# A layer's output stage: who turns the gated attention rows, TensorE or a transposing DMA, and roots taken for two row tiles at once

## The chip, the cores and the metric

The kernel runs on one core of one Trainium2 chip. The metric is device time in microseconds (us) of one execution; the median of three runs is given. A core has TensorE (PE in the profile; its weight loads are PEld), VectorE (DVE), ScalarE (ACT), GpSimd (POOL) and the queue engine SyncE (SP), which here issues most transfers. Each engine runs its own instructions in order; they wait for one another through semaphores.

## The reference, cut to what matters

A hybrid decoder layer for 2048 positions of width 1024. Two attention branches (8 heads with a forget gate, 8 heads in a sliding window) fill one row `o` of 1024 values for each position. The last stage then gates, projects, normalises and adds:

```
oa = oa * silu(za); ob = ob * silu(zb)
y = concatenate([oa, ob], axis=-1) @ w_out      # 2048x1024 @ 1024x1024
x = x + gate * rms_norm(y, g_post)              # root over the 1024 values of a row
```

## The kernel before, in words

All products are made in half precision parts: a number is split into a high f16 part and the f16 rest, and three matmuls (high-high, high-low, low-high) stand for one.

The attention leaves its rows in memory tensor `o_d` (positions by channels) and the gates in `z_d` (channels by positions, 8 blocks of 128). The output stage works in 16 row tiles of 128 positions, class `Out`, one object `outs[t]` for each. A tile's life:

- `load` (SP queue): `z` (L1457) and then `o` (L1451), 512 KB each, into quarters of the buffer `T`, two tiles in rotation.
- `turn`: eight 128x128 TensorE transposes (L1463) put `o`, channels first, into two PSUM banks. Then, each some ticks later: `gate` (DVE, L1472, two multiplies of 512 columns, PSUM times `z`, into `z`), `squares_` (ACT, L1475, sum of squares of `z`), `scale_` (a TensorE matmul with `ones` to add over partitions, L1479, then the two small DVE operations of `root_scale`, L112 and L113), the high part (ACT, L1485) and the low part (DVE, L1486) of the scaled `z`, which are the stationary operand `hl` (tile `oz`) of the product.
- `product(n, k)`: half `n` (512 output columns) of the product, for channel block `k`; three matmuls of 512 columns (L1499). 16 such units make a tile: 48 matmuls. After unit `k` = 7 of a half, `evac`: ACT squares the PSUM bank with a row sum (L1507), DVE multiplies it with the gate row into `y` (L1515).
- `root`: fifteen DVE operations on one column (`unscale` L1525 and L1526, L1543 and L1544, `rsqrt_mean` L92 to L106 with three Newton steps, L1546). `store`: one DVE operation over 1024 columns (L1553) adds `x`, and SP writes 512 KB out (L1554). `x` is loaded at the first unit of the second half (L1496).

The order is written out by hand. `ounits` lists the units: the products of tiles 0 and 1, then for each tile t from 2 on the 16 products in order, with `turn` of tile t+1 behind the third. `after(n, f)` puts `f` into a list; each `tick()` counts the entries down and calls those that are due, in the order in which they were put there. In the final part a tick follows every second unit. Python order is instruction order on each engine:

```
def tick():
    now = [f for n, f in late if n <= 1]
    late[:] = [[n - 1, f] for n, f in late if n > 1]
    for f in now:
        f()
```

The first `N_IN` = 33 units (tiles 0 and 1 and the turn of tile 2) are mixed into the last head of the attention; the rest, from tile 2 on, run alone. "Host tile" below is the tile whose products run while the turn of the next tile goes on in their midst.

`rsqrt_mean(dst, ss, n)` works on `n` columns; its Newton step is two operations for `n` = 1 and three for larger `n`. Another place of the kernel, the sliding window attention, already uses transposing DMAs: `Pair.split` writes a high and a low f16 part of 128x1024 and sends each through `SP.dma_start_transpose` (L908, L913).

Of the kernel before, what the change touches and what calls it, by code (L numbers as in the profile page):

```python
# [15 lines left out]
ALU = mybir.AluOpType  # L16
AX = mybir.AxisListType

P = 128
# [21 lines left out]
def hybrid_layer(  # L41
# [1347 lines left out]
    def open_out():  # L1389
# [9 lines left out]
        def rotate(key, views):  # L1399
            n = [0]  # L1400

            def next_():
                n[0] += 1
                return views[n[0] % 2]

            oio[key] = next_
# [6 lines left out]
        rotate("x", oxy[:2])  # L1413
        rotate("y", oxy[2:])
        oio["w"] = wo.tile([P, 2, KT, D], F16, name="wohl")
# [20 lines left out]
    class Out:  # L1436


        def __init__(self, t):
            self.t = t  # L1440
            self.last = t == NB - 1
            self.cuts = (0, CH, CH + 3 * P, D) if self.last else (0, CH, D)

# [9 lines left out]
        def load_z(self):  # L1453
# [3 lines left out]
            SP.dma_start(self.z, z_d[:, :, rows_].rearrange("k p n -> p k n"))  # L1457

        def turn(self, lag):

            px = [bk[bank()][:].rearrange("p (k n) -> p k n", k=4) for _ in range(2)]
            for k in range(KT):
                PE.transpose(px[k // 4][:, k % 4, :], self.o[:, k * P:(k + 1) * P], ident[:])  # L1463
            self.hl = wpool.tile([P, 2, KT, P], F16, tag=("whl", "wraw")[self.t % 2], name="oz")
            self.sc = sm(1, "w_pw")
            hi, lo = self.hl[:, 0], self.hl[:, 1]
            gs = sm(1, "w_mx")

            def gate():
                for h in range(2):  # L1470
                    z = self.z[:, 4 * h:4 * h + 4, :]
                    V.tensor_tensor(z, px[h], z, op=ALU.mult)  # L1472

# [3 lines left out]
            def scale_():  # L1477
                pg = bk[bank()][:, 0:1]
                PE.matmul(pg, ones[:], gs[:], start=True, stop=True)  # L1479
                root_scale(self.sc[:], pg)  # L1480

            after(1, gate)
            after(2, squares_)
            after(lag, scale_)
            after(lag + 1, lambda: A.activation(hi, self.z, AF.Copy, scale=self.sc[:]))  # L1485
            after(lag + 2, lambda: V.scalar_tensor_tensor(lo, self.z, self.sc[:], hi, op0=ALU.mult, op1=ALU.subtract))  # L1486

        def product(self, n, k):
            cc = slice(self.cuts[n], self.cuts[n + 1])
            if k == 0:  # L1490
                self.b = bank(True)
                if n == 0:
                    self.ss = sm(4, "y_ss")
                elif n == 1:
                    self.x = oio["x"]()
                    SP.dma_start(self.x[:], xs[self.t * P:(self.t + 1) * P, :])  # L1496
            py, b = bk[self.b][:, :cc.stop - cc.start], self.b
# [21 lines left out]
            if n == len(self.cuts) - 2:  # L1519
                after(2 if self.last else 4, self.root)  # L1520
                after(2 if self.last else 7, self.store)

        def unscale(self):
            self.inv = sm(1, "w_sw")
            V.tensor_tensor(self.inv[:], self.sc[:], ysc[:], op=ALU.mult)  # L1525
            V.reciprocal(self.inv[:], self.inv[:])  # L1526
# [8 lines left out]
        def root(self):  # L1535
# [4 lines left out]
            else:  # L1540
# [5 lines left out]
                V.tensor_tensor(rst[:], rst[:], inv[:], op=ALU.mult)  # L1546
            self.rst = rst

        def store(self):
            y, rst = self.y, self.rst  # L1550
            for n, e in enumerate((SP, A) if self.last else (SP,)):
                cc = slice(n * CH, (n + 1) * CH) if self.last else slice(0, D)
                V.scalar_tensor_tensor(y[:, cc], y[:, cc], rst[:], self.x[:, cc], op0=ALU.mult, op1=ALU.add)  # L1553
                e.dma_start(os_[self.t * P:(self.t + 1) * P, cc], y[:, cc])  # L1554
# [4 lines left out]
    for t, n in [(0, 0), (1, 0), (0, 1), (1, 1)] + [(t, n) for t in range(2, NB) for n in range(len(outs[t].cuts) - 1)]:  # L1559
        if n == 0 and t + 2 < NB:  # L1560
            oloads[len(ounits)] = t + 2
        for q in range(KT):
            ounits.append(lambda t=t, n=n, q=q: outs[t].product(n, q))
            nxt = 2 if (t, n) == (0, 1) else t + 1 if n == 0 and 2 <= t < NB - 1 else None
            if q == 2 and nxt:
                ounits.append(lambda nxt=nxt: outs[nxt].turn(4))
    opos = [0]
    N_IN = 4 * KT + 1

# [156 lines left out]
```

## Time and profile before

| | |
|---|---|
| median of 3 runs (lowest, highest) | 1167.06 us (1166.04, 1169.31) |
| the profiled execution | 1165.92 us, span 1164.2 us |
| mean granted TensorE clock | 0.995 |
| busy share of the span | PE 96%, DVE 79%, ACT 58%, POOL 14% |
| TensorE operations L1463 in the last stage | 128x128, f32 |
| bytes of one execution | 136.36 MB over DMA, 117 GB/s in the mean |

The span reaches from the first to the last instruction; the rest of the execution's time lies around it. Busy time of PE is no measure of the end by itself, since matmuls overlap; the chain of work that ended last says where time passes.

### The profile page before, as it was taken

Reading aid. Unit: us, or ns where it says so; the run is one execution under the profiler, and the core shown is the slowest. Engines: PE = TensorE matmul, PEld = TensorE weight load, DVE = VectorE, ACT = ScalarE, POOL = GpSimd, SP = SyncE. Lnnn points to the kernel's source line nnn. Section 1 sums busy time; section 2 is a strip of 40 time slices with the busy share of each in tenths; the row PEclk is TensorE's granted clock in tenths of the full one; section 3 lists DMA queues with packets and bytes.
Section 4 is the critical chain, followed back from the end, with each engine's and each line's share of the span. In section 5 each row is a group of like instructions: output and inputs, shape, how many; then the busy total and the mean of one; then the engine's idle time right before and its main releaser. Section 6 shows DMA issues by size and latency. Waiting matters only on the chain. (4 is left out here: it accounts for less than half of the span.)

```text
span 1164.2 us, 27013 instructions
## 1 busy us (share of the span) xinstructions
PE 1116.3 (96%) x10514; PEld 652.8 (56%) x10514; DVE 915.9 (79%) x2330; ACT 677.9 (58%) x1124; POOL 166.0 (14%) x302
## 2 busy tenths in 40 slices
PE   5899999999999999999999999999999989999997
PEld 1466557544469955555555555555555555555554
DVE  6776578889878757789988889878897886767665
ACT  4666445656545534767766667777676688323332
POOL 2011223233332201111111111002000000000000
PEclk9999999999999999999999999999999999999999
DMA  9645446576766622333233232313112255454642
GB/s 330 219 139 166 106 76 134 116 162 129 147 134 130 123 64 69 85 83 79 74 77 92 73 79 74 68 42 94 45 45 49 60 169 172 150 201 166 211 165 89
DMA packets 162452, 136.36 MB, mean 117 GB/s; under 512 B 95356, under 2 KB 139428, under 8 KB 162324
## 3 DMA queue, kind: packets, MB, share of 16 engines
q1 hardware_dynamic: 152388, 106.39, 34.8%
q0 software_dynamic: 9456, 27.72, 8.9%
q8 instruction: 82, 1.34, 0.5%
q10 hardware_dynamic: 480, 0.53, 0.2%
q14 instruction: 46, 0.38, 0.1%
HBM read 70.97 MB, written 25.18 MB: 83 GB/s over the span
## 5 line engine op out<-in xcount | busy, mean ns | idle before, releaser
L1331 ACT ACTIVATE p<-sta,lift,scl_qk 128x1024 f32<-128x1024 f32 (+2 forms) x160 | 171.8, 1074 | 94.7 <-PE sta L1327 88.9
L334 PE MATMUL bk<-hT,wh_qk 128*128 128x512 f16 x768 | 197.9, 378 | 0.6 <-DVE a_m L1280 0.6
L1499 PE MATMUL bk<-wohl,oz 128*128 128x512 f16 (+2 forms) x792 | 172.5, 372 | 2.2 <-DVE oz L1486 1.0
L1342 DVE TENSOR_TENSOR pha<-p,pha 128x1024 f16<-128x1024 f32 (+2 forms) x160 | 169.8, 1061 | 0.0
L1339 ACT ACTIVATE pha<-p 128x1024 f16<-128x1024 f32 (+2 forms) x160 | 148.1, 925 | 31.6 <-POOL p L1335 26.8
L1280 DVE TENSOR_REDUCE a_m<-bk 128x1 f32<-128x512 f32 x192 | 129.4, 684 | 36.2 <-PE bk L1277 35.3
L1499 PEld LDWEIGHTS <-oz 128*128 128x128 f16 x792 | 75.8, 99 | 83.2 <-issue 1.8
L1352 PE MATMUL poa<-vt,pha 128*128 128x65 f16 x1088 | 116.5, 193 | 1.6 <-DVE ona L1361 1.6
L1355 PE MATMUL poa<-vt,pha 128*128 128x65 f16 x1088 | 116.0, 192 | 1.4 <-DVE pha L1342 1.4
L1354 PE MATMUL poa<-vt,pha 128*128 128x64 f16 x1088 | 116.3, 194 | 0.0
L1326 PE MATMUL sta<-T 128*128 128x512 f16 (+1 forms) x320 | 109.6, 347 | 4.5 <-ACT p L1331 4.5
L1277 PE MATMUL bk<-T 66*128 66x512 f16 (+2 forms) x320 | 110.5, 348 | 2.1 <-DVE a_m L1280 2.1
L1352 PEld LDWEIGHTS <-pha 128*128 128x128 f16 x1088 | 101.6, 97 | 16.3 <-DVE ona L1361 2.9
L334 PEld LDWEIGHTS <-wh_qk 128*128 128x128 f16 x768 | 70.2, 97 | 71.6 <-issue 2.9
L1354 PEld LDWEIGHTS <-pha 128*128 128x128 f16 x1088 | 101.0, 97 | 13.4
L1327 PE MATMUL sta<-T 69*128 69x512 f16 (+1 forms) x320 | 108.0, 348 | 0.0
L1355 PEld LDWEIGHTS <-pha 128*128 128x128 f16 x1088 | 100.8, 99 | 1.6 <-DVE pha L1342 1.6
L334 PE MATMUL bk<-hT,wh_za 128*128 128x512 f16 x384 | 99.9, 379 | 0.0
L352 PE MATMUL bk<-wh_va,hT 128*128 128x128 f16 x1536 | 94.1, 221 | 0.0
L352 PEld LDWEIGHTS <-hT 128*128 128x128 f16 x1536 | 89.1, 99 | 6.1 <-issue 3.3
L334 PE MATMUL bk<-hT,wh_zb 128*128 128x512 f16 x384 | 91.2, 379 | 1.0 <-DVE wh_zb L278 1.0
L1335 POOL TENSOR_SCALAR_AFFINE_SELECT p<-p 128x256 f32<-128x256 f32 x64 | 31.9, 499 | 413.4 <-ACT p L1331 408.5
(497 smaller groups left out, 1857.0 us busy)
## 6 DMA issues: line engine op xcount, KB each, us to landing
hT<-in_x_dram SPq DMA_DIRECT2D x20, 512.0 KB
wa<-in_w_ada_dram SPq DMA_DIRECT2D x16, 512.0 KB
T<-stq SPq DMA_DIRECT2D x128, 64.0 KB
T<-z_d SPq DMA_DIRECT2D x16, 512.0 KB
T<-o_d SPq DMA_DIRECT2D x16, 512.0 KB
z_d<-tz POOLq DMA_DIRECT2D x30, 256.0 KB, 2.9
out_dram<-hT SPq DMA_DIRECT2D x15, 512.0 KB
xt<-in_x_dram SPq DMA_DIRECT2D x12, 512.0 KB
```

What stands on the lines that cost most here:

```text
L334: PE.matmul(ps, whl[:, a, k, :], hT[ci][:, b, k, :], start=(k == 0 and n == 0), stop=(k == KT - 1 and n == 2))
L352: PE.matmul(ps[:, u * P:(u + 1) * P], hT[ci][:, a, k, u * P:(u + 1) * P], whl[:, b, k, :], start=(k == 0 and n == 0), stop=(k == KT - 1 an ...
L1277: PE.matmul(mx[:, :w], T[0:XM, 0, i * P:(i + 1) * P], T[0:XM, 2, pc * CH:pc * CH + w], start=True, stop=True)
L1280: V.tensor_reduce(m3[:, u, pc:pc + 1], mx[:, :w], axis=AX.X, op=ALU.max)
L1326: PE.matmul(self.st[:, o:o + w], T[:, 3, kb_], T[:, 1, qc], start=True, stop=False)
L1331: A.activation(self.p32[:, :self.w], self.st[:, :self.w], AF.Exp, scale=scl[f"qk{self.hd}"][:], bias=lift[:])
L1339: A.activation(self.ph[:, 0, :self.w], self.p32[:, :self.w], AF.Copy)
L1342: V.tensor_tensor(self.ph[:, 1, :self.w], self.p32[:, :self.w], self.ph[:, 0, :self.w], op=ALU.subtract)
L1352: PE.matmul(po[:, u, :], ph[:, 0, pq], vt[:, b, hd, 0:65], start=(self.first and n == 0 and u == 0), stop=False)
L1354: PE.matmul(po[:, u, 0:64], ph[:, 0, pq], vt[:, b, hd, 65:VW], start=False, stop=False)
L1355: PE.matmul(po[:, u, :], ph[:, 1, pq], vt[:, b, hd, 0:65], start=False, stop=(self.last and n == len(self.blocks) - 1))
L1499: PE.matmul(py, self.hl[:, i, k, :], w_slot(8 * j + k)[:, cc], start=(k == 0 and m_ == 0), stop=(k == KT - 1 and m_ == 2))
```

## The change: what it does

For tiles 3 to 15, `turn` issues no TensorE transposes. A new unit, `split` of tile t+2, stands behind the second product unit of the second half of tile t (t from 1 to 13): ACT copies `o` into a f16 high part, DVE subtracts it from `o` for the f16 low part (at the next tick), and SP sends each part, 128x1024, through a transposing DMA into one half of a buffer `tt`; both are two tiles in rotation, as views of the tile `spare`. `gate` becomes two DVE operations over 1024 columns: `o` = high + low (f16 and f16, f32 out), then `z` = `o` * `z`.

For tiles 2 to 13, the roots are taken in pairs (`pair_root`, 3 ticks after the odd tile's last product; 19 DVE operations on two columns, `rsqrt_mean` with `n` = 2), and the two stores follow 5 and 7 ticks after that product. Both tiles' `x` loads are issued in the odd tile, and `y` gets a third buffer. `N_IN` is 34, since `split` of tile 3 lies in the mixed part. With `split`, a tile has 18 units, so 9 ticks.

```diff
--- before.py
+++ after.py
@@ -1401,7 +1401,7 @@
 
             def next_():
                 n[0] += 1
-                return views[n[0] % 2]
+                return views[n[0] % len(views)]
 
             oio[key] = next_
 
@@ -1411,7 +1411,10 @@
         oio["r"] = [spare[:, 2 * CH * n:2 * CH * (n + 1)].bitcast(F32) for n in range(6)]
         oio["j"] = [spare[:, CH * a:CH * b].bitcast(BF16) for a, b in ((12, 14), (14, 15), (15, 16))]
         rotate("x", oxy[:2])
-        rotate("y", oxy[2:])
+        rotate("y", oxy[2:] + [gz[:]])
+        turned = [spare[:, 4 * CH * n:4 * CH * (n + 1)].rearrange("p (a k q) -> p a k q", a=2, k=KT) for n in range(2)]
+        rotate("t", turned)
+        oio["s"] = spare[:, 8 * CH:12 * CH].rearrange("p (a n) -> p a n", a=2)
         oio["w"] = wo.tile([P, 2, KT, D], F16, name="wohl")
 
         fm = sm(1, "w_p2")
@@ -1439,6 +1442,7 @@
         def __init__(self, t):
             self.t = t
             self.last = t == NB - 1
+            self.paired = 2 <= t < NB - 2
             self.cuts = (0, CH, CH + 3 * P, D) if self.last else (0, CH, D)
 
         def load(self):
@@ -1456,20 +1460,40 @@
             self.z = Ts[0][:, 2 + t % 2, :].bitcast(F32).rearrange("p (k n) -> p k n", k=KT)
             SP.dma_start(self.z, z_d[:, :, rows_].rearrange("k p n -> p k n"))
 
+        def split(self):
+            hl, self.tt = oio["s"], oio["t"]()
+
+            def low():
+                V.tensor_tensor(hl[:, 1, :], self.o, hl[:, 0, :], op=ALU.subtract)
+                SP.dma_start_transpose(self.tt[:, 1], hl[:, 1, :])
+
+            A.activation(hl[:, 0, :], self.o, AF.Copy)
+            SP.dma_start_transpose(self.tt[:, 0], hl[:, 0, :])
+            after(1, low)
+
         def turn(self, lag):
 
-            px = [bk[bank()][:].rearrange("p (k n) -> p k n", k=4) for _ in range(2)]
-            for k in range(KT):
-                PE.transpose(px[k // 4][:, k % 4, :], self.o[:, k * P:(k + 1) * P], ident[:])
+            mate = self.t - 1 if 2 < self.t < NB - 2 and self.t % 2 else None
+            self.pair = outs[mate].pair if mate else (sm(4, "b_m"), sm(4, "b_nb"))
+            e = self.t % 2
             self.hl = wpool.tile([P, 2, KT, P], F16, tag=("whl", "wraw")[self.t % 2], name="oz")
-            self.sc = sm(1, "w_pw")
+            self.sc = self.pair[0][:, e:e + 1] if self.paired else sm(1, "w_pw")[:]
             hi, lo = self.hl[:, 0], self.hl[:, 1]
             gs = sm(1, "w_mx")
+            if self.t < 3:
+                px = [bk[bank()][:].rearrange("p (k n) -> p k n", k=4) for _ in range(2)]
+                for k in range(KT):
+                    PE.transpose(px[k // 4][:, k % 4, :], self.o[:, k * P:(k + 1) * P], ident[:])
 
             def gate():
-                for h in range(2):
-                    z = self.z[:, 4 * h:4 * h + 4, :]
-                    V.tensor_tensor(z, px[h], z, op=ALU.mult)
+                if self.t < 3:
+                    for h in range(2):
+                        z = self.z[:, 4 * h:4 * h + 4, :]
+                        V.tensor_tensor(z, px[h], z, op=ALU.mult)
+                else:
+                    o = self.o.rearrange("p (k n) -> p k n", k=KT)
+                    V.tensor_tensor(o, self.tt[:, 0], self.tt[:, 1], op=ALU.add)
+                    V.tensor_tensor(self.z, o, self.z, op=ALU.mult)
 
             def squares_():
                 A.activation(oio["j"][0].rearrange("p (k n) -> p k n", k=KT), self.z, AF.Square, accum_out=gs[:])
@@ -1477,23 +1501,24 @@
             def scale_():
                 pg = bk[bank()][:, 0:1]
                 PE.matmul(pg, ones[:], gs[:], start=True, stop=True)
-                root_scale(self.sc[:], pg)
+                root_scale(self.sc, pg)
 
             after(1, gate)
             after(2, squares_)
             after(lag, scale_)
-            after(lag + 1, lambda: A.activation(hi, self.z, AF.Copy, scale=self.sc[:]))
-            after(lag + 2, lambda: V.scalar_tensor_tensor(lo, self.z, self.sc[:], hi, op0=ALU.mult, op1=ALU.subtract))
+            after(lag + 1, lambda: A.activation(hi, self.z, AF.Copy, scale=self.sc))
+            after(lag + 2, lambda: V.scalar_tensor_tensor(lo, self.z, self.sc, hi, op0=ALU.mult, op1=ALU.subtract))
 
         def product(self, n, k):
             cc = slice(self.cuts[n], self.cuts[n + 1])
             if k == 0:
                 self.b = bank(True)
                 if n == 0:
-                    self.ss = sm(4, "y_ss")
-                elif n == 1:
-                    self.x = oio["x"]()
-                    SP.dma_start(self.x[:], xs[self.t * P:(self.t + 1) * P, :])
+                    self.ss = self.pair[1][:, 2 * (self.t % 2):2 * (self.t % 2) + 2] if self.paired else sm(4, "y_ss")[:]
+                    if self.paired and self.t % 2:
+                        outs[self.t - 1].load_x()
+                elif n == 1 and (self.t % 2 or not self.paired):
+                    self.load_x()
             py, b = bk[self.b][:, :cc.stop - cc.start], self.b
             for m_, (i, j) in enumerate(((0, 0), (0, 1), (1, 0))):
                 PE.matmul(py, self.hl[:, i, k, :], w_slot(8 * j + k)[:, cc],
@@ -1517,12 +1542,35 @@
 
             after(1, evac)
             if n == len(self.cuts) - 2:
-                after(2 if self.last else 4, self.root)
-                after(2 if self.last else 7, self.store)
+                if not self.paired:
+                    after(2 if self.last else 4, self.root)
+                    after(2 if self.last else 7, self.store)
+                elif self.t % 2:
+                    mate = outs[self.t - 1]
+                    after(3, self.pair_root)
+                    after(5, mate.store)
+                    after(7, self.store)
+
+        def load_x(self):
+            self.x = oio["x"]()
+            SP.dma_start(self.x[:], xs[self.t * P:(self.t + 1) * P, :])
+
+        def pair_root(self):
+            sc, ss = self.pair[0][:, 0:2], self.pair[1]
+            inv, s = sm(4, "b_rs")[:, 0:2], sm(4, "b_ri")[:, 0:2]
+            V.tensor_scalar(inv[:], sc, ysc[:], None, op0=ALU.mult)
+            V.reciprocal(inv[:], inv[:])
+            V.tensor_reduce(s[:], ss[:].rearrange("p (t h) -> p t h", t=2), axis=AX.X, op=ALU.add)
+            V.tensor_tensor(s[:], s[:], inv[:], op=ALU.mult)
+            V.tensor_tensor(s[:], s[:], inv[:], op=ALU.mult)
+            rst = sm(4, "a_m4")[:, 0:2]
+            rsqrt_mean(rst, s, 2)
+            V.tensor_tensor(rst[:], rst[:], inv[:], op=ALU.mult)
+            outs[self.t - 1].rst, self.rst = rst[:, 0:1], rst[:, 1:2]
 
         def unscale(self):
             self.inv = sm(1, "w_sw")
-            V.tensor_tensor(self.inv[:], self.sc[:], ysc[:], op=ALU.mult)
+            V.tensor_tensor(self.inv[:], self.sc, ysc[:], op=ALU.mult)
             V.reciprocal(self.inv[:], self.inv[:])
 
         def part(self):
@@ -1544,13 +1592,13 @@
                 V.tensor_scalar(ss[:, 0:1], ss[:, 0:1], inv[:], inv[:], op0=ALU.mult, op1=ALU.mult)
                 rsqrt_mean(rst, ss[:, 0:1], 1)
                 V.tensor_tensor(rst[:], rst[:], inv[:], op=ALU.mult)
-            self.rst = rst
+            self.rst = rst[:]
 
         def store(self):
             y, rst = self.y, self.rst
             for n, e in enumerate((SP, A) if self.last else (SP,)):
                 cc = slice(n * CH, (n + 1) * CH) if self.last else slice(0, D)
-                V.scalar_tensor_tensor(y[:, cc], y[:, cc], rst[:], self.x[:, cc], op0=ALU.mult, op1=ALU.add)
+                V.scalar_tensor_tensor(y[:, cc], y[:, cc], rst, self.x[:, cc], op0=ALU.mult, op1=ALU.add)
                 e.dma_start(os_[self.t * P:(self.t + 1) * P, cc], y[:, cc])
 
     outs = [Out(t) for t in range(NB)]
@@ -1564,8 +1612,10 @@
             nxt = 2 if (t, n) == (0, 1) else t + 1 if n == 0 and 2 <= t < NB - 1 else None
             if q == 2 and nxt:
                 ounits.append(lambda nxt=nxt: outs[nxt].turn(4))
+            if q == 1 and n == 1 and t and t + 2 < NB:
+                ounits.append(lambda t=t: outs[t + 2].split())
     opos = [0]
-    N_IN = 4 * KT + 1
+    N_IN = 4 * KT + 2
 
     def ofill(n, each=None):
         for _ in range(n):
```

## The prediction

> **What bounds the kernel now.** I read the page first, for the busy shares, then the chain of work that ended last over the final 160 us, where the change lies, then the timeline there.
>
> ```profile
> span 1164.2 us, 27013 instructions
> PE 1116.3 (96%) x10514; PEld 652.8 (56%) x10514; DVE 915.9 (79%) x2330; ACT 677.9 (58%) x1124; POOL 166.0 (14%) x302
> ```
>
> The chain (start, length, what):
>
> ```profile
> 1011.72 0.87 PE bk L1463 x8
> ...
> 1050.71 6.50 PE bk L1499 x30
> 1057.20 0.87 PE bk L1463 x8
> 1058.08 4.53 PE bk L1499 x21
> 1062.61 0.12 PE bk L1479 x2
> ...
> 1068.57 0.87 PE bk L1463 x8
> ...
> 1136.79 0.87 PE bk L1463 x8
> ```
>
> From tile 3 to tile 14 the chain holds TensorE alone: no wait is in it. A matmul takes 6.50/30 = 0.217 us, a tile 48 of them = 10.40, plus 0.87 for eight transposes and 0.12 for the scale's matmul: 11.39, and the rows of the transposes are 11.37 apart. Twelve groups of transposes stand between 1011.72 and 1136.79. The other engines in five of these slices (columns: time, PE, PEld, DVE, ACT, POOL busy, clock, DMA share, GB/s):
>
> ```profile
> 1100.00:1150.00 50.00, 50.00 (x255) 25.35 (x254) 33.52 (x106) 15.38 (x30) 0.00 (x0) 1.00 0.48 162
> ```
>
> So DVE has a third of its time left, ACT two thirds, DMA half: on average. The change must be read tile by tile.
>
> **What goes.** Thirteen tiles lose 0.87 us of TensorE each: 11.3 us, all of it on the path. If nothing took its place, that would be the result.
>
> **What DVE gets.** The durations (busy total, mean ns, idle before), and the one place of this stage where a root already runs ahead of a gate, in tile 2:
>
> ```profile
> L1515 DVE TENSOR_TENSOR hT<-bk,gacc 128x512 f32<-128x512 f32 x30 | 20.7, 691 | 32.9 <-ACT hT L1507 32.9
> L1486 DVE SCALAR_TENSOR_TENSOR oz<-T,w_pw,oz 128x1024 f16<-128x1024 f32 x16 | 20.5, 1282 | 1.4 <-ACT oz L1485 1.2
> L1472 DVE TENSOR_TENSOR T<-bk,T 128x512 f32<-128x512 f32 x30 | 19.3, 685 | 10.9 <-PE bk L1463 10.9
> L1553 DVE SCALAR_TENSOR_TENSOR hT<-hT,y_rs 128x1024 f32<-128x1024 f32 x15 | 19.1, 1275 | 0.0
> L1342 DVE TENSOR_TENSOR pha<-p,pha 128x1024 f16<-128x1024 f32 x8 | 9.7, 1215 | 0.0
> ```
>
> ```profile
> 999.52 0.15 DVE L1525 TENSOR_TENSOR w_sw<-w_pw,ysc 128x1 f32<-128x1 f32 x1
> ...
> 1002.32 1.29 DVE L1472 TENSOR_TENSOR T<-bk,T 128x512 f32<-128x512 f32 x2
> ...
> 1003.64 1.06 ACT L1475 ACTIVATE hT<-T 128x1024 bf16<-128x1024 f32 x1 [7.80 <-DVE T L1472]
> ...
> 1004.84 0.38 PE L1479 MATMUL bk<-w_mx,ones 128*128 128x1 f32 x2 [0.42 <-ACT hT L1475]
> ...
> 1005.64 1.15 ACT L1485 ACTIVATE oz<-T,w_pw 128x1024 f16<-128x1024 f32 x1 [0.28 <-DVE w_pw L113]
> ```
>
> Fifteen root operations run from 999.52 to 1002.32: 0.187 us each, though they hold one column. After the gate's end (1002.32 + 1.29 = 1003.61) come squares and the scale's matmul; that ends at 1005.22. So TensorE goes on 1.61 us after the gate's end, and the small scale operations cost about 0.4 more before the high part.
>
> Step by step, for DVE:
> - `pair_root`: 19 operations. Two columns instead of one are nothing beside such a fixed cost, so 19 x 0.187 = 3.55 us for two tiles, where two roots took 5.60. DVE gains 2.05 us a pair, but all 3.55 now stand in one tile.
> - The gate: 2 x 0.685 = 1.37 go. The multiply of 1024 f32 columns is nearest to L1342: 1.215. The addition reads two f16 operands and writes f32; no row has that. Its ends are 1.28 (L1486, the slowest of this width) and 0.61 (half of L1342, if two half-width operands ran at twice the rate). L1342 already reads one f16 operand and writes f16 at the usual rate, so I take 1.215. Gate: 2.43, so 1.06 more.
> - The low part of `split`: f32 minus f16 to f16 over 1024 columns is L1342's form: 1.215.
>
> The Trainium skill, "VectorE: DVE Perf Modes", section "What auto-detection actually checks", says that the double rate of a two-operand operation needs every tensor to be 16-bit; the f32 result rules it out here. By the other case the sum below would be 0.6 us a tile lower.
>
> **Where these stand in the queue.** `pair_root` is put on the list in the odd tile's last unit and falls due at the third tick, after the even tile's unit 3, a tick in which the gate is due too. It was listed first, so DVE runs it before the gate. Before, the root was due one tick later and ran behind the gate. Evacuation of the tile boundary:
>
> ```profile
> 1055.36 0.60 ACT L1507 ACTIVATE hT<-bk 128x512 bf16<-128x512 f32 x1 [3.08 <-PE bk L1499]
> 1055.85 0.19 ACT L1507 ACTIVATION_READ_ACCUMULATOR hT<-bk 128x1 f32 x1
> 1056.08 0.69 DVE L1515 TENSOR_TENSOR hT<-bk,gacc 128x512 f32<-128x512 f32 x1 [1.98 <-ACT hT L1507]
> ```
>
> The boundary B, end of the old tile's last matmul, is 1050.71 + 21 x 0.217 = 1055.26; DVE starts the last evacuation at B+0.82 and is free at B+1.51. An even host tile then goes so:
> - pair root to B+5.06, gate to B+7.49, TensorE past the scale's matmul at B+9.10.
> - TensorE reaches that matmul after 9 units, 27 x 0.217 = B+5.85, and would be past it at B+5.97. Everything of `product` queues behind it: a stall of 3.13 us.
> - 21 more matmuls, 4.55: the tile ends at B+13.65, where it took 11.37: +2.28.
> - DVE meanwhile: store of the even partner (1.275) to 8.77, scale operations to 9.5, evacuation to 10.2, second store to 11.5, low part of `split` to 12.7, low part of `oz` to 14.0. The next product's third matmul wants the latter at 13.65 + 0.43 = 14.08: just in time.
>
> The order is not the whole of it. DVE's work in this tile, 0.69 + 3.55 + 2.43 + 1.275 + 0.35 + 0.69 + 1.275 + 1.215 + 1.28 = 12.75, begun at B+0.82, ends at B+13.6 at best; a tile without a stall wants it at 10.40 + 0.12 + 0.43 = 10.95. In any order of the queue the pair loses 2.6 us and gains 2 x 0.87.
>
> **What the transfers do.** Two transposes of the size needed, from the sliding window part: SP's issues, then DMA busy tenths in slices of 0.1 us from 382 us on with what they moved:
>
> ```profile
> 381.60 1.23 SPq L908 DMA_TRANSPOSE ptb<-sp  x1
> 382.89 1.32 SPq L913 DMA_TRANSPOSE ptb<-sp  x1
> ```
>
> ```profile
> DMA  9730000169999999999997899999999997310000
> q1 hardware_dynamic: 2085, 0.52, 68.0%
> ```
>
> Both (0.52 MB) run from 382.8 to 385.4: 2.6 us together, and the second has landed 2.5 us after its issue began. SP spends 1.3 us on each issue.
>
> The Trainium skill, "VectorE: DVE Perf Modes", section "The three transpose paths", speaks against the change: 1309 ns for a 128x128 block by DMA and 390 by TensorE. Sixteen blocks a tile one after the other would be an estimated 20.9 us, twice a tile, some 130 us over thirteen tiles; the 2.6 us for sixteen blocks above disagree, and the measurement decides.
>
> Loads and stores of one tile (slices of 0.3 us from 1051.5 on):
>
> ```profile
> DMA  0000000599984967999999999999710000000000
> q1 hardware_dynamic: 1472, 2.10, 52.0%
> 1054.13 0.37 SPq L1457 DMA_DIRECT2D T<-z_d  x1
> 1054.59 0.67 SPq L1451 DMA_DIRECT2D T<-o_d  x1
> ```
>
> 2.10 MB take 52% of 12 us, 6.2 us; with 2.6 it is 8.8 of a tile's 10.5: DMA fits. `o` is behind `z` and the old store; the whole burst is over by 1060.5, B+5.2, and `split`'s copy falls at B+6.8 or later: covered. In an even tile the low part is written at B+12.7, its transpose lands at 15.2 alone, or at 15.9 if half of the second store's 512 KB is ahead of it. The odd tile begins at 13.65, its gate could run at 15.16. So its gate is 0.1 to 0.75 late, and of that TensorE, which has 5.97 - (1.51 + 2.43 + 1.61) = 0.42 spare, feels 0 to 0.35; I take 0.2. ACT's copy of 1.06 is covered by ACT's two idle thirds, the moved `x` loads by a whole tile before their stores. On SP the low part's transpose waits for DVE at 12.7; behind it stand the next `z` and `o` loads, which wait for the low part of `oz` at 14.0 anyway. `split` of tile 3 is in the mixed part, where ACT and DVE are fuller: 0 if hidden, 1.2 if all of it (one low part) shows; I take 0.5. A gain there has no source.
>
> **The clock.** A gap of TensorE has been costly once (stretches, PE busy first, granted clock third from the end):
>
> ```profile
> 47.70:51.11 3.41, 1.98 (x9) 0.66 (x7) 3.34 (x6) 3.35 (x6) 0.00 (x0) 1.00 0.08 19
> 51.11:54.53 3.42, 2.62 (x33) 1.84 (x32) 3.17 (x13) 2.17 (x5) 0.00 (x0) 1.00 0.02 6
> 341.25:344.66 3.41, 1.35 (x24) 0.83 (x23) 3.34 (x12) 2.80 (x10) 0.60 (x1) 1.00 0.68 142
> 344.66:348.07 3.41, 3.41 (x41) 3.41 (x38) 3.29 (x10) 0.00 (x0) 2.11 (x4) 0.50 0.64 119
> ```
>
> 3.41 us with 1.35 busy were followed by 3.41 us at half clock; 3.41 with 1.98 busy were not. A stall of 3.1 leaves such a stretch under half busy in most positions. Half clock for 3.41 us costs up to 1.7; part of it falls into the stall itself, so I take 1.4 for six of the seven stalls (tile 2 has one too, 0.42 + 0.87 + 1.06 = 2.35). It also makes the odd tile begin later, which hides the late transposes.
>
> **The sum**, against the profiled execution's 1165.92 (the median of the runs, 1167.06, is 1.1 above it): six even host tiles (4 to 14) x 2.28 = +13.7; five odd ones (5 to 13) without transposes, -0.87 + 0.2 = -0.67, -3.3; tile 3 -0.9; tile 2, whose gate follows a single root, +1.06; `split` of tile 3 +0.5: +11.1. Clock: 6 x 1.4 - 5 x 0.2 = +7.4. Together +18.5: 1184.4 us.
>
> **Rivals.**
> - Stalls without the half clock: TensorE waits as above, but no stretch falls under the limit, which the rows only bound between 1.35 and 1.98 busy. 1165.92 + 11.1 = 1177. The Trainium skill, "TensorE: Matmul & The Clock Gate", section "Why this matters for your kernels", warns of idle gaps above about 3 us; the gap in the stretch at 341.25 was 3.41 - 1.35 = 2.06, and the clock fell, so this trace is stricter than the page.
> - Faster: DVE has room after all. Place: the even tile's pair root and gate; price: the stall of 3.13. If the small operations overlap and the addition runs at 0.61, the stall shrinks; it decides below 1.5 us a pair, where the transposes' 1.74 is worth more; with none it is 1165.92 - 11.3 = 1154.6. For it: 33.52 of 50 us busy. Against it: 12.75 us in one tile.
> - Late transposes: the low part's transpose waits behind two stores and, in odd tiles, four 512 KB loads follow. Each us later costs 1 us in six odd tiles; 1 to 2 us give 1190 to 1196. For it: 8.8 of 10.5 us of DMA. Against it: the burst is over 5 us before the tile's end.
> - No change: stalls of just 1.7 us a pair cancel the gain, 1166.
>
> **How the numbers follow.** Forecast with half clock 0.53, without it 0.26, late transposes 0.08, faster 0.07, no change 0.06. What a measurement here can tell from no change is 0.3%, 3.5 us. Low end: no half clock, and the addition at 0.61 in seven tiles, 1177 - 4.2 = 1172.8, so 1172; high end: 1.7 for all seven, odd stalls of 0.35 and 1.2 for tile 3, 1177 + 11.9 + 0.8 + 0.7 = 1190.4, so 1191. Faster 0.07, same 0.06, slower 0.87.
>
> **What will show it.** Right: no L1463 rows after tile 2's; waits of TensorE at the scale's matmul for ACT's squares, about 3 us in even host tiles, near 0 in odd ones; tile lengths alternating near 13.7 to 15 and 10.5; pair roots of 3.5 us directly ahead of the two gate operations; half-clock stretches after the stalls. Wrong: a gate that runs before the root, an addition near 0.6 us, DVE waits for `tt` above 1 us, or equal tiles of 10.5.

## The result, and the profile after

The changed kernel takes 1187.43 us (median of 4 runs, 1185.18 to 1189.15), the kernel before 1166.55 in the same comparison: a ratio of 1.0175, 95% interval [1.0159, 1.0192]. So it is 1.75% slower, some 20.9 us. The profiled execution took 1186.93 us, with a span of 1185.2 us. From its page:

```profile
PE 1116.9 (94%) x10410; PEld 642.6 (54%) x10410; DVE 933.5 (79%) x2277; ACT 688.1 (58%) x1137; POOL 166.2 (14%) x302
...
PEclk9999999999999999999999999999999999999988
```

TensorE has 104 matmuls less, as the change says, DVE's busy share is 79% as before. That TensorE's share falls from 96% to 94%, and that the last two digits of the clock are 8, is all the page shows of the problem. The loss is seen in the last stage. TensorE's waits from 985 us on (line waiting, what it waited for: us in total, times, longest) now have a row that the kernel before had only once, 0.4 us in tile 2:

```profile
PE bk L1503 <- ACT hT L1499: 20.8, 9, 2.7
```

Each tile has one scale's matmul (L1479 before, L1503 after), so its starts measure the tiles. Before, the first and the last two of the stretch, then after, from tile 2 on:

```profile
1016.97 0.28 PE L1479 MATMUL bk<-w_mx,ones 128*128 128x1 f32 x2
...
1130.67 0.28 PE L1479 MATMUL bk<-w_mx,ones 128*128 128x1 f32 x2
1141.39 0.28 PE L1479 MATMUL bk<-w_mx,ones 128*128 128x1 f32 x2
```

```profile
1006.04 0.38 PE L1503 MATMUL bk<-w_mx,ones 128*128 128x1 f32 x2 [2.48 <-ACT hT L1499]
1018.33 0.28 PE L1503 MATMUL bk<-w_mx,ones 128*128 128x1 f32 x2
1031.71 0.38 PE L1503 MATMUL bk<-w_mx,ones 128*128 128x1 f32 x2 [2.72 <-ACT hT L1499]
1043.55 0.38 PE L1503 MATMUL bk<-w_mx,ones 128*128 128x1 f32 x2 [1.07 <-ACT hT L1499]
1057.04 0.38 PE L1503 MATMUL bk<-w_mx,ones 128*128 128x1 f32 x2 [2.73 <-ACT hT L1499]
...
1147.57 0.28 PE L1503 MATMUL bk<-w_mx,ones 128*128 128x1 f32 x2
1160.95 0.58 PE L1503 MATMUL bk<-w_mx,ones 128*128 128x1 f32 x2 [2.73 <-ACT hT L1499]
```

The five pairs of tiles between 1018.33 and 1147.57 take 25.85 us each; before they took (1130.67 - 1016.97)/5 = 22.74. The interval that ends at an even host tile's matmul is 13.4 to 13.5 with a wait of 2.7; the odd ones are 11.7 to 13.7. The timeline of one even host tile (tile 6; start, us, engine, line; idle before in brackets):

```profile
1049.91 0.22 DVE L1561 TENSOR_SCALAR b_rs<-b_m,ysc 128x2 f32<-128x2 f32 x1
...
1053.18 0.16 DVE L1568 TENSOR_TENSOR a_m<-a_m,b_rs 128x2 f32<-128x2 f32 x1
1053.26 1.23 DVE L1495 TENSOR_TENSOR T<-hT 128x1024 f32<-128x1024 f16 x1
1054.52 1.22 DVE L1496 TENSOR_TENSOR T<-T 128x1024 f32<-128x1024 f32 x1
...
1055.84 1.06 ACT L1499 ACTIVATE hT<-T 128x1024 bf16<-128x1024 f32 x1 [6.57 <-DVE T L1496]
1057.28 12.21 PE L1524 MATMUL bk<-wohl,oz 128*128 128x512 f16 x48
```

The pair's root stands directly ahead of the gate. It takes 3.35 us (1049.91 to 1053.26), the gate 2.48, ACT has been idle for 6.57 us when it gets the squares, and TensorE stands for 2.73. Then 48 matmuls take 12.21 us instead of 10.4. The reason is in the clock (stretch, PE busy first, granted clock third from the end):

```profile
1003.40:1006.90 3.50, 1.02 (x6) 0.54 (x6) 2.97 (x6) 2.06 (x5) 0.00 (x0) 1.00 0.64 225
1006.90:1010.30 3.40, 3.40 (x10) 1.26 (x9) 2.92 (x3) 1.65 (x2) 0.00 (x0) 0.53 0.82 234
1054.70:1058.10 3.40, 1.06 (x6) 0.63 (x7) 2.85 (x5) 2.26 (x5) 0.00 (x0) 1.00 0.12 40
1058.10:1061.50 3.40, 3.40 (x10) 1.23 (x9) 3.40 (x4) 1.45 (x2) 0.00 (x0) 0.53 1.04 157
...
1133.20:1136.60 3.40, 2.75 (x8) 1.31 (x9) 2.64 (x6) 3.16 (x6) 0.00 (x0) 0.53 0.39 157
1136.60:1140.00 3.40, 3.40 (x9) 1.21 (x8) 2.36 (x3) 0.00 (x0) 0.00 (x0) 0.50 1.07 276
```

With two more, from 1109.3 and from 1160.5 us on, these are six stretches of 3.4 us at half clock, behind five of the seven stalls. A granted clock of 0.53 over 3.40 us from 1006.90 means that the half clock began 0.2 us into the row. So worked out, it began at 1007.1, 1058.3, 1109.5, 1133.4 and 1160.7 us: 15, 15, 7 and 8 steps of 3.41 us apart. In these traces the clock changes on a grid of such steps, and it matters how a stall lies on it. The five stalls left 0.9 to 1.3 us of a step busy; the other two, in tiles 4 and 8, are split over two steps, and no half clock followed. Tile 4's:

```profile
1027.60:1031.00 3.40, 1.39 (x7) 0.42 (x5) 3.30 (x6) 0.49 (x1) 0.00 (x0) 1.00 0.01 4
1031.00:1034.40 3.40, 2.69 (x14) 1.39 (x15) 2.84 (x6) 3.22 (x6) 0.00 (x0) 1.00 0.39 155
```

Why the half clock from 1133.4 lasted two steps and the others one is not shown. A stretch costs about 1.7 us, as the chain shows with 12.07 us for 48 matmuls that take 10.38 at full clock (row with e3 below):

```profile
1108.56 12.07 PE bk L1524 x48
```

Where no such stretch delays the odd tile, its gate finds the low part not yet turned. Tile 5:

```profile
1035.43 1.52 SPq L1468 DMA_TRANSPOSE hT<-hT  x1
...
1039.77 1.22 DVE L1495 TENSOR_TENSOR T<-hT 128x1024 f32<-128x1024 f16 x1 [1.61 <-DMA hT<-hT]
```

That transpose landed 4.3 us after its issue began (4.7 and 4.1 in tiles 7 and 9, where the gate waited too), and TensorE waited 1.07 us for it at 1043.55.

### The profile page after: what moved, and what is told of

The parts are those of the page before. It is cut to its first block, busy times and chain, and to the rows that moved or that the text cites. A ratio compares the mean times of both kernels' runs of the same rounds, so it can differ in the third digit from the quotient of the medians.

```text
span 1185.2 us, 26840 instructions
## 1 busy us (share of the span) xinstructions
PE 1116.9 (94%) x10410; PEld 642.6 (54%) x10410; DVE 933.5 (79%) x2277; ACT 688.1 (58%) x1137; POOL 166.2 (14%) x302
## 4 chain that ended last, share of the span: by engine, by line
PE 67%; DVE 14%; ACT 7%; DMA 6%; issue 4%; SPq 1%; POOL 0%; ACTq 0%; DVEq 0%; POOLq 0%
PE bk L334 26%; PE bk L1524 8%; PE bk L352 7%; PE bk L1277 5%; PE sta L1326 4%; PE sta L1327 4%; PE poa L1354 3%; PE poa L1352 2%; PE poa L1355 2%; DMA wa<-in_w_ada_dram 2%; PE bk L774 1%; DMA T<-o_d 1%; DVE sp L912 1%; PE pss L865 1%; PE pob L928 1%
## 5 line engine op out<-in xcount | busy, mean ns | idle before, releaser
L1524 PE MATMUL bk<-wohl,oz 128*128 128x512 f16 (+2 forms) x792 | 179.6, 387 | 1.8 <-DVE oz L1510 1.0
L1524 PEld LDWEIGHTS <-oz 128*128 128x128 f16 x792 | 78.2, 102 | 93.3 <-issue 13.9
L334 PE MATMUL bk<-hT,wh_qb 128*128 128x512 f16 x384 | 89.4, 379 | 1.3 <-DVE wh_qb L278 1.3
```

The lines of the kernel that those rows point to most:

```text
L334: PE.matmul(ps, whl[:, a, k, :], hT[ci][:, b, k, :], start=(k == 0 and n == 0), stop=(k == KT - 1 and n == 2))
L1524: PE.matmul(py, self.hl[:, i, k, :], w_slot(8 * j + k)[:, cc], start=(k == 0 and m_ == 0), stop=(k == KT - 1 and m_ == 2))
```

## The experiments

Theory: DVE's order in the even tile, the pair's root of 3.35 us ahead of the gate, stalls TensorE, and the half clock multiplies it. Rivals: the transposing DMAs themselves are the price; or DVE has simply too much work in that tile, in whatever order. All ratios are against the kernel before on the same chip; its median was 1166.3 to 1167.0 on each of them, so medians of different runs are set side by side too.

**One part each.** `e1_single_roots` takes the pairs away, `e2_pairs_only` the transposing DMAs.

```diff
# e1_single_roots
-            self.paired = 2 <= t < NB - 2
+            self.paired = False
# e2_pairs_only (and no split units)
-            if self.t < 3:
+            if True:
                 px = ...
```

> Transposing DMA kept, roots single again as before the change (due one tick after the gate). Theory 1, DVE's queue in the even tile makes the stall: the gate runs ahead of the root, so no wait at the scale's matmul from it; DVE has 0.69 + 2.43 + 2.80 + 0.35 + 0.69 + 1.28 + 1.22 + 1.28 = 10.7 us in each tile, done at B+11.6 where 10.95 is wanted: about 0.6 us a tile lost against 0.87 gained, 1163 to 1167 us, no half clock. Rival, the transposes land too late: they are all still there, so most of the loss stays, 1180 or more.

Measured: 1173.91 us (1171.13 to 1175.8), ratio 1.0056 [1.0039, 1.0073]. Between the two, and 7 us above what the theory gave: the transposes alone do not gain 11 us, they lose 6.5. TensorE's waits:

```profile
PE bk L1521 <- DVE oz L1507: 6.2, 11, 0.6
PE bk L1500 <- ACT hT L1496: 5.5, 11, 2.5
```

The first row is the 0.6 us a tile that was expected. The second, apart from the 2.5 in tile 2, was not; it comes from the gate's own wait. The timeline of one tile:

```profile
1068.88 1.29 SPq L1468 DMA_TRANSPOSE hT<-hT  x1
...
1072.19 1.23 DVE L1492 TENSOR_TENSOR T<-hT 128x1024 f32<-128x1024 f16 x1 [1.54 <-DMA hT<-hT]
```

The low part lands 3.3 us after issue. It is made behind the store on DVE, which stands behind the root, which stands behind the gate: gate, root, scale, store, low part, transpose, next gate form a ring of 11.8 us a tile, longer than TensorE's 10.5.

> Pair roots and their stores as in the change, TensorE transposes for all tiles, no split. Theory 1: in even tiles the pair root runs ahead of the gate, gate ends at B+6.4, TensorE goes on at B+8.0 where it was due at 6.84: a stall of 1.2 in six tiles, too short for the half clock: 1174 us. Rival, late transposes: no transposing DMA here, so nothing is lost and 1166 us stay.

Measured: 1172.81 (1170.92 to 1173.43), ratio 1.0043 [1.0026, 1.0059], as the theory has it, though with stalls of 0.7 us where it had 1.2. The wait is there without any transposing DMA, but short, since the gate is shorter and TensorE comes later by its transposes:

```profile
PE bk L1503 <- ACT hT L1499: 4.4, 7, 0.7
```

The two parts cost 0.56% and 0.43% alone and 1.75% together. Only together do the stalls of the even tiles grow to 2.7 us, and most of those are followed by half clock.

**The half clock.** `e3_fill` lets TensorE do useless matmuls where it would stand.

```diff
+                if self.t > 2 and self.t % 2:
+                    for _ in range(12):
+                        PE.matmul(b_[:], identh[:], w_slot(0)[:, 0:CH], start=True, stop=True)
                 PE.matmul(pg, ones[:], gs[:], start=True, stop=True)
```

> The changed kernel with 12 matmuls of no use (512 columns, into the bank of the scale's sum, which overwrites what is read) put on TensorE's queue ahead of the scale's matmul of the odd tiles, 2.6 us of work inside stalls of 2.7 to 3.1 us. Half clock as a cause: the half-clock stretches of the host stage (20.5 us recorded, worth 10.2 at full speed) go, odd tiles begin earlier and see some more of the late transposes, 1178 to 1182 us although work was added. If the half clock costs nothing: 1187 or more.

Measured: 1180.57 (1178.97 to 1182.09), ratio 1.0114 [1.0099, 1.0129]: 6.9 us less than the changed kernel, though DVE does the same and TensorE more. The twelve matmuls take 2.59 us in the chain, about the whole stall, and the 48 behind them run at full clock:

```profile
1004.27 2.59 PE bk L1506 x12
1007.14 10.38 PE bk L1528 x48
```

What remains are the stalls themselves and the late transposes of the odd tiles (waits of DVE, then of TensorE):

```profile
DVE T L1495 <- DMA hT<-hT: 6.9, 5, 2.2
...
PE bk L1507 <- ACT hT L1499: 4.5, 5, 1.9
```

**The transposes' lateness.** In `e4_no_wait` the transposes are sent, but nobody waits for them.

```diff
-                    V.tensor_tensor(o, self.tt[:, 0], self.tt[:, 1], op=ALU.add)
+                    hl = oio["s"].rearrange("p a (k n) -> p a k n", k=KT)
+                    V.tensor_tensor(o, hl[:, 0], hl[:, 1], op=ALU.add)
```

> The changed kernel, but the gate adds the two parts before they are turned, from the buffer that the transposes read; the transposes are still sent, and nobody waits for them (the output is that of unturned rows). Theory 1: only the waits of DVE for the transposes go, 3.6 us in three odd tiles, of which TensorE felt about 1: 1184 to 1187 us. Rival, late transposes are the cause: 1170 or less.

Measured: 1178.38 (1173.78 to 1182.1), ratio 1.0094 [1.0066, 1.0122]; 9 us less than the changed kernel: more than the theory had, less than the rival. Part of it is the clock: the profiled execution (1182.1) has three half-clock stretches instead of six. A pair of tiles takes 24.0 us here, seven steps of the grid, and four stalls in a row lie split over two steps (2.2 and 1.9 us busy around the one of 1034.48). The fastest run had a mean clock of 0.997 beside the profiled one's 0.991. Two intervals of the profiled one, even and odd host tile:

```profile
1034.48 0.38 PE L1504 MATMUL bk<-w_mx,ones 128*128 128x1 f32 x2 [2.72 <-ACT hT L1500]
1045.08 0.28 PE L1504 MATMUL bk<-w_mx,ones 128*128 128x1 f32 x2
...
1058.47 0.38 PE L1504 MATMUL bk<-w_mx,ones 128*128 128x1 f32 x2 [2.73 <-ACT hT L1500]
```

The odd tile takes 10.60 us (the changed kernel's tile 5: 11.84), the even one 13.39 with its stall untouched. From tile 2's matmul (1008.82) to the end this execution takes 7.6 us less than the changed kernel's; three stretches of 1.7 are 5.1 of it, and the rest, 2.5, is put down to the lateness of the transposes (tiles 5 and 9 alone, 11.84 and 11.65 against 10.60, give 2.3). Ahead of tile 2's matmul it lost 2.8 us. I have no cause for that; in the other kernels that are the same up to there, this matmul starts between 1005.15 and 1006.76.

**Order or load.** `e5_gate_first` moves the pair's root behind the gate; `e6_spread` also moves the stores on. (In these two and in `e8_early_pool`, the rows of tile 12 take tile 14's `x`, since its load then stands ahead of tile 12's store.)

```diff
-                    after(3, self.pair_root)
-                    after(5, mate.store)
-                    after(7, self.store)
+                    after(4, self.pair_root)
+                    after(6, mate.store)      # e6_spread: 9
+                    after(8, self.store)      # e6_spread: 13
```

> The changed kernel with pair root and both stores one tick later, so that DVE runs the gate of an even tile ahead of the pair root; nothing else. If the order in DVE's queue is the whole cause: no wait at the scale's matmul, 1160 to 1168 us (late transposes left). Theory 1, DVE has 12.75 us of work in the even tile in any order: the wait moves from the scale's matmul to the low part of oz, about 2.6 us in six tiles, some of them with half clock, 1178 to 1184 us.

Measured: 1177.24 (1174.73 to 1179.81), ratio 1.0094 [1.0076, 1.0113], just under the 1178 to 1184 that the load gives: this order alone is not enough. The wait moved from the scale's matmul to the low part of `oz`, which now stands behind root and stores:

```profile
PE bk L1524 <- DVE oz L1510: 12.2, 6, 2.4
```

> Gate ahead of the pair root as in the run before, and the two stores moved out of DVE's full stretch: the even partner's to the end of the even tile, the odd partner's into the odd tile behind its gate. DVE's work in the even tile is 10.2 us then. Theory 1: the large stalls and the half clock go; what is left is the low part's transpose, written at B+9.8 of the even tile and late by about 1.5 us in odd tiles: 1160 to 1168 us. If DVE's load in the even tile isn't the cause: 1178 or more.

Measured: 1169.4 (1168.26 to 1172.14), ratio 1.0031 [1.002, 1.0042], 18 us less than the changed kernel with the same work, and 1.4 above the expected range. So the load of 12.75 us in one tile could be spread. What is left is mostly the lateness of the transposes (DVE's waits, then TensorE's, 2.5 us of them in tile 2, behind the single root):

```profile
DVE T L1495 <- DMA hT<-hT: 11.1, 10, 2.7
...
PE bk L1503 <- ACT hT L1499: 8.6, 10, 2.5
```

**Two misses with GpSimd.** To break the ring of `e1_single_roots`, `o` is loaded half a tile earlier, split earlier, and the low part made on GpSimd: on e6 (`e8_early_pool`) and on single roots (`e9_single_early_pool`).

```diff
-            if q == 1 and n == 1 and t and t + 2 < NB:
+            if (q, n) == ((0, 0) if t > 2 else (1, 1)) and t and t + 2 < NB:
                 ounits.append(lambda t=t: outs[t + 2].split())
+            if (q, n) == (6, 0) and 2 <= t and t + 3 < NB:
+                ozs[len(ounits)] = t + 3          # o of tile t+3 is loaded here
...
-                V.tensor_tensor(hl[:, 1, :], self.o, hl[:, 0, :], op=ALU.subtract)
+                (G if self.t > 4 else V).tensor_tensor(hl[:, 1, :], self.o, hl[:, 0, :], op=ALU.subtract)
```

> As the run before, and from tile 5 on the rows o are loaded half a tile earlier, the split stands behind the first product unit of a tile, and its low part is computed by GpSimd, idle in this stage (about 2.5 us for 1024 columns by its 1.27 for 512): the transposes have 6 us until the gate. DVE's work is 10.3 us in an even tile, 9.9 in an odd one. Theory 1 with late transposes as its second term: no stall of TensorE is left from tile 4 on, 1155 to 1159 us, faster than before. If another limit stands behind (DMA or DVE slowed by GpSimd): 1163 or more.

> Transposing DMA with single roots, the early load and split, and the low part on GpSimd: 9.5 us of DVE in every tile, done at B+10.35 where 10.95 is wanted, transposes early. Theory 1 and late transposes as its second term: 1155 to 1159 us without any pairing; so the roots' pairing gains nothing of its own. If pairing is what lets DVE keep up: slower than the run before by 3 us or more.

Measured: 1208.57 (ratio 1.0363 [1.0348, 1.0379]) and 1195.3 (1.0255 [1.0238, 1.0272]). Both theories failed, for two reasons. First, the split unit ahead of `turn` moved `turn` one unit on, so that gate and root fell due in one tick, the root listed first; in e8 TensorE waited at the scale's matmul in every tile from 2 to 13:

```profile
PE bk L1503 <- ACT hT L1499: 33.4, 12, 4.0
```

Second, DVE stood still beside GpSimd. From e8's timeline:

```profile
1073.21 2.88 POOL L1467 TENSOR_TENSOR hT<-T,hT 128x1024 f16<-128x1024 f32 x1 [14.36 <-ACT hT L1470]
1074.02 3.15 DVE L1495 TENSOR_TENSOR T<-hT 128x1024 f32<-128x1024 f16 x1
...
1085.82 2.12 POOL L1467 TENSOR_TENSOR hT<-T,hT 128x1024 f16<-128x1024 f32 x1 [9.73 <-ACT hT L1470]
1085.95 2.01 DVE L1564 TENSOR_TENSOR b_ri<-b_ri,b_rs 128x2 f32<-128x2 f32 x1
```

The addition, 1.23 us alone, takes 3.15 and ends 1.08 after GpSimd's operation; an operation on two columns takes 2.01 and ends with it. The Trainium skill, "SBUF — State Buffer", section "SBUF: two separate sides", says that VectorE operations with two SBUF inputs and GpSimd operations take a shared port pair in turn, each for its whole length; these rows agree. Operations with one source were not held up: in e9, five of them on one column, 0.14 to 0.27 us each, ran within one GpSimd subtraction (1069.64 to 1071.77), and the first with two sources, at 1070.63, took 1.15 and ended with it. The two reasons were not tried apart.

**A version that is faster than both.** `e10_evac_later` keeps GpSimd out and changes the order alone: `o` early, `split` right behind `turn`, the root behind gate and low part, the stores in two different tiles, the second half's evacuation behind the next gate.

```diff
-            if q == 1 and n == 1 and t and t + 2 < NB:
+            if (q, n) == ((2, 0) if t > 2 else (1, 1)) and t and t + 2 < NB:
...
-                    after(3, self.pair_root)
-                    after(5, mate.store)
-                    after(7, self.store)
+                    after(5, self.pair_root)
+                    after(8 if self.t == 13 else 9, mate.store)
+                    after(11 if self.t == 13 else 16, self.store)
...
-            after(1, evac)                    # e11_even_queue keeps this line
+            after(4 if n == 1 and self.paired else 1, evac)
```

> The changed kernel with another order and nothing else. o of a tile is loaded half a tile earlier (behind the gate that frees its buffer), split stands right behind the turn unit, so both transposes are issued a tile ahead of their gate; the pair's root runs two ticks later, behind the gate and the low part; the two rows' stores follow in two different tiles, the loads of x move with them; and the second half's evacuation of a paired tile runs behind the next gate. Theory (order and late transposes held the time, and a pair's 19.4 us of VectorE fit its 21.0 us of TensorE): 1155 to 1160 us, no wait of VectorE for the transposed halves, waits of TensorE at the scale's matmul and for oz's low part under 1 us each over the whole stage. Rival (VectorE's load itself is too much, as in e5_gate_first): 1166 to 1172, with waits for oz's low part of some 6 us or more in sum.

Measured: 1162.25 (1160.01 to 1164.3), ratio 0.9961 [0.9947, 0.9974]: faster than before by 0.4%, and 25 us faster than the changed kernel, with the same arithmetic. It stays 2 us above the expected range. The scale's matmuls, and TensorE's waits:

```profile
1017.22 0.28 PE L1503 MATMUL bk<-w_mx,ones 128*128 128x1 f32 x2
...
1090.70 0.28 PE L1503 MATMUL bk<-w_mx,ones 128*128 128x1 f32 x2
1101.63 0.38 PE L1503 MATMUL bk<-w_mx,ones 128*128 128x1 f32 x2
```

```profile
PE bk L1503 <- ACT hT L1499: 2.7, 2, 2.5
```

The seven tiles between the first two rows take (1090.70 - 1017.22)/7 = 10.50 us each, which is 48 matmuls, the scale's, and no wait. The stall in tile 2 (2.5) is left, and the four tiles from 1090.70 on take 10.9 to 11.8, where `o` and the transposed halves are late again.

> As e10_evac_later, but the second half's evacuation stays ahead of the next gate, as in the kernel before. Theory: the odd tile's gate then begins only when the pair's first store and this evacuation are done, some 2.2 to 2.6 us after the tile's boundary, where 1.9 us would still do: 0.3 to 0.7 us of waiting at the scale's matmul in each of six odd tiles, 2 to 4 us in sum, so 1158 to 1164 us. Rival (the order at the boundary does not matter, since TensorE has slack there): within 1 us of e10_evac_later.

Measured: 1164.56 (1162.46 to 1165.89), ratio 0.9977 [0.9969, 0.9986]: 2.3 us above e10, at the lower end of the 2 to 4 us that the theory gave (the range in time was missed by 0.6 us, since e10 itself stood above its own). The waits at the scale's matmul, in e10 almost only that of tile 2, come back in small: 6.0 us in 7, of which 2.5 in tile 2.

> e10_evac_later with the single root of tile 1 one tick later, so that it runs behind the gate of tile 3 instead of ahead of it. In e10_evac_later that gate began at 1001.86 us, right behind the root's 2.9 us, and TensorE waited 2.5 us at the scale's matmul; 48 matmuls after it took 1.1 us longer than elsewhere. Theory: the wait of 2.5 us and the slow matmuls behind it both go, so 3 to 4 us less: about 1158 to 1160 us. Rival (another wait takes its place, for example the scale operations behind the root): above 1161 us, with a wait at oz's low part in the same tile.

Measured: 1162.9 (1161.01 to 1164.4), ratio 0.9965 [0.9951, 0.9979], no change against e10. One tick later the root falls due together with the gate and still runs first; the stall of 2.5 is there. The edit missed its aim.

> e10_evac_later with the single root of tile 1 two ticks later and its store two ticks later, so that the gate of tile 3 runs ahead of this root (in e12_tile2 one tick was not enough: root and gate fell due together, the root had been listed first, and the wait of 2.5 us stayed). Theory: the gate then runs from about 999.1 to 1001.6 us and TensorE passes the scale's matmul near 1003.2; the wait of 2.5 us goes, and with it the half clock behind it (45 matmuls in 11.42 us, where 48 take 10.38 to 10.40 elsewhere): 3 to 4 us less than e10_evac_later, so 1158 to 1160 us, a ratio near 0.993. Rival (the 2.5 us come back as another wait in the same tile, at oz's low part, or in the next): 1161 us or more.

```diff
-                    after(2 if self.last else 4, self.root)
-                    after(2 if self.last else 7, self.store)
+                    after(2 if self.last else 6 if self.t == 1 else 4, self.root)
+                    after(2 if self.last else 9 if self.t == 1 else 7, self.store)
```

Measured: 1163.09 (1160.48 to 1164.97), ratio 0.9972 [0.9962, 0.9983]: the rival. Its timeline and chain:

```profile
1003.29 0.28 PE L1503 MATMUL bk<-w_mx,ones 128*128 128x1 f32 x2
...
1006.48 1.06 ACT L1470 ACTIVATE hT<-T 128x1024 f16<-128x1024 f32 x1 [2.84 <-DMA T<-o_d]
```

```profile
1017.61 12.06 PE bk L1522 x48
```

The gate ran earlier, and TensorE passed that matmul without a wait. But the copy for tile 4's split had to wait for `o` as well, its transposes came no earlier, and the stall stands one tile on (the waits' row: 2.4 us), with half clock behind it. So the three versions are one time within what can be told, and e10 stands for them.

## Why the prediction was right, point by point

The forecast was 1184.4 us; 1187.43 was measured, and 1186.93 in the profiled execution. By stretches between the scale's matmuls, profiled executions:

| stretch | before | after | more | predicted |
|---|---|---|---|---|
| start to tile 2's matmul | 1004.84 | 1006.04 | +1.2 | +1.06 + 0.5 |
| to tile 3's | 12.13 | 12.29 | +0.2 | -0.9 + 1.4 |
| five pairs | 113.70 | 129.24 | +15.5 | 5 x (2.28 - 0.67 + 1.4 - 0.2) = +14.1 |
| to tile 14's | 10.72 | 13.38 | +2.7 | +2.28 |
| to the end | 22.81 | 24.25 | +1.4 | 0 |
| sum | 1164.2 | 1185.2 | +21.0 | +18.4 |

(The prediction's own sum, rounded at each step, is +18.5.) Before, the interval was 10.72 and 12.02 us in turn, since 17 units are eight and a half ticks; so a row of a single tile is uncertain by 0.65 us, and the row of pairs is the one to read. Its 15.5 us are nearly accounted for: the stalls, 1.25 a pair (e4's pairs of 23.99 us against 22.74), are 6.3, four stretches at half clock of 1.7 are 6.8, the late tiles 5 and 9 are 2.3. The prediction had 7.1, 7.0 and nothing in sum. That the total came so near owes something to luck: the stalls came out shorter, and the lateness longer.

- The pair's root ahead of the gate: right in place. It takes 3.35 us instead of 3.55, and the stall is 2.73 instead of 3.13. The interval that ends in an even host tile took 13.38 to 13.49, against 13.65 for such a tile.
- The f16 addition at the full 1.22 us: right. All thirteen:

```profile
L1495 DVE TENSOR_TENSOR T<-hT 128x1024 f32<-128x1024 f16 x13 | 15.9, 1222 | 3.6 <-DMA hT<-hT 3.6
```

- The half clock: right in mechanism. Predicted 7.4 net; removing it gave 6.9 (e3). It was to follow six of seven stalls, once each; it followed five, once twice. The last lies after tile 14's matmul, in the table's last row, where I had none. The Trainium skill, "TensorE: Matmul & The Clock Gate", section "Why this matters for your kernels", names gaps above about 3 us; here gaps of 2.5 to 2.7 did it, so the measurement is stricter. By the page's rule, stalls as short as these would have cost no half clock, which is the rival at 1177, 10 us too low.
- The odd tiles: the step that was mis-sized. I took the transpose of the low part to land 2.5 us after its issue, as in the sliding window, and the lateness as 0.2 us a tile. It landed after 4.1 to 4.7 us in tiles 5, 7 and 9, and one of the signs of being wrong came with it: DVE waited more than 1 us for `tt` in two tiles (1.61 and 1.42). Where the half clock does not hide it (e3), TensorE waits 4.5 us for it over five odd tiles; beside the half clock 2.3 us remain. Why the transpose took longer was not isolated: it was issued among loads and stores on the same queue. The odd host tiles took 11.7 to 13.7 us instead of near 10.5, by the half clock and by this. This is the rival "late transposes", priced at 1 us a tile; I gave it a small chance as a case of its own, and it came as a part of the likeliest.
- "In any order of the queue the pair loses 2.6 us" was wrong. I counted the work of the even tile as bound to it. A pair holds, by the prediction's own durations, 19.4 us of DVE work (four evacuations 2.76, root 3.55, two each of gate 4.86, store 2.55, scale 0.7, low parts 2.43 and 2.56) and 21.0 of TensorE's. e10 put one store into the odd tile and the evacuations behind the gates, and most of its tiles took 10.50 us. The predicted floor of the rival "faster", 1154.6, holds; with the right order the change is worth 4.6 us, with the order it came in it costs 20.9.
- The load of `o` being covered was right for the changed kernel (ACT's copy waited for it once, 0.3 us). In e10's last tiles (1085 to 1141 us) and in e13 the copies do wait for it, and some gates for the transposed halves; how much each costs there was not tried apart. ACT's waits in e10's last tiles, then DVE's in its whole stage, of which 3.1 us are in tile 3, where TensorE did not feel it:

```profile
ACT hT L1470 <- DMA T<-o_d: 12.2, 4, 6.3
...
DVE T L1495 <- DMA hT<-hT: 8.3, 4, 3.1
```

## What to carry to other kernels

When work is bundled (two roots at once), ask in whose queue the whole bundle now stands and what is behind it: a saving of 2 us in the sum became a stall of 2.7 in one tile. An average with a third of an engine free says nothing about that tile, but it does say that an order may exist in which the work fits; look for it before giving up the idea. When two things fall due in the same tick, the order in which they were listed decides, and adding one unit elsewhere can change it.

## What the runs showed of the hardware that was not expected

- Stalls of 2.5 to 2.7 us were enough for 3.4 us at half clock when they lay in one step of the grid of 3.41 us. In the last stage of all fourteen kernels, every step at full clock with up to 1.35 us busy was followed by half clock and none with 1.6 or more; in between both occurred (1.41 in the changed kernel without, 1.57 in e13 with). With such stalls filled with 2.59 us of useless matmuls (e3) the whole took 6.9 us less.
- A transposing DMA of 128x1024 f16 that landed in 2.5 us in the sliding window took 3.3 us (e1) and 4.1 to 4.7 us (after) among loads and stores on the same queue.
- DVE operations with two sources did not run beside a two-source GpSimd operation (e8): 2.01 us instead of 0.16 for two columns, 3.15 instead of 1.22 for 1024. Those with one source did (e9).
